# Tying the modulation row sums to the five-tap convolution that precedes them

## Chip, core and metric

The kernel runs on one core of a Trainium2 chip. The metric is the device time of one launch in microseconds (us), the median of three runs. The engines are TensorE (PE, matrix products; PEld is its weight load), VectorE (DVE), ScalarE (ACT), GpSimd (POOL) and SyncE (SP, which here issues most DMA transfers).

## The reference

One layer of a diffusion backbone over 512 latent tokens of width 1024 and 256 context tokens. Cut to its shape:

```
mod = silu(c) @ w_ada + b_ada        # 6 chunks of 1024: shift, scale, gate, shift, scale, gate
h   = modulate(rms_norm(x), shift1, scale1)
z, xbc, dt, conv_in, pool_in, gates = split(h @ w_in)
y_ssd  = bidirectional_ssd(silu(depthwise_conv5(xbc)), softplus(dt + bias)) * silu(z)
y_conv = silu(layer_norm(depthwise_conv31(glu(conv_in))))
y_pool = multi_scale_pool(pool_in)
x = x + gate1 * (merge(y_ssd, y_conv, y_pool, sigmoid(gates)) @ w_out)
x = x + gate2 * swiglu(modulate(rms_norm(x), shift2, scale2))
out = rms_norm(x)
```

The change touches the part of `mod` that isn't needed for `h`: chunks 2, 4 and 3 (gate1, scale2, shift2), 24 row blocks of 128 outputs. Each is a sum over 1024 inputs, `sum(w_ada_row * silu(c)) + b_ada`, worked out on DVE.

## The kernel before

Weights are stored as 128 x 1024 blocks. `load_unit` (L116) brings one in on SP's queue (`wr`, three buffers, L113), ACT casts it to `whi` (L121), DVE takes the rest as `wlo` (L123), and PE multiplies it with the activations in three matmuls per 128 rows (L135 to L137, `mm3`), 24 matmuls of 128x512 for a unit of 512 tokens.

The stages follow one another on PE as: the convolution branch's inputs (`glu_pair`), the pooling branch, the dt block (`dt_all`, L594 on), twelve units of xbc with the five-tap convolution (`conv5`, L673; DVE taps at L677), then the units of z and of the branch gates (`spill_tile`, `gate_tiles`), in which the SSD chunks (`ssd_gen`, L780) are mixed, then the projections `wcv`, `wso`, `wout` and the feed-forward part.

The dt block: DVE makes dt by a chain on tiles of 128x192 (L621 to L624), then dta (L628) and its logs (L631); PE takes dta at L638 to L641 and L655. An SSD chunk: PE makes C.B (L819), ACT copies it (`cbs`, L821), PE applies the states (L832, L836), DVE scales and adds (L833, L837 to L839), masks and multiplies the decays (L854, L857), PE transposes and adds into one bank (`y`, L846 and L859), DVE multiplies with the gate (L866), ACT squares (L868), DVE adds (L869, L870), PE averages (L872).

The 31-tap convolution of the second branch, `conv31` (L391), is 180 steps on DVE (L403) on three pairs of tiles, A_456, A_457 and A_458. `conv_steps` issues so many of them at a place. `cv_norm` (L424) sums the six tiles (`sum`, L427 and L429) and gives the sum to PE (mean matmul L430), which needs one bank for that.

The order is not that of the text. A scheduler takes, on each engine, what its estimate says is ready, by priority; a block under `later(n)` has a lower one. `tc.issue_after(ins)` gives the instructions under it an edge in issue order alone: they come behind `ins` on their engine, and do not wait for its end elsewhere. `mark` is a list that starts with a small copy and to which every five-tap step is appended (L677 to L680); `conv_steps(n, mark[-1])` already uses it for the 31-tap steps.

The 24 row sums are made by `ada`: it first reduces what has been loaded (`ada_rest`, L733, the reduction at L736 with a read of the accumulator), then takes the next row block and loads its 512 KB (`ar`, two buffers, L747, on SP's queue). It is called once in each xbc unit from the fourth on, after `conv_steps`, then once for every second unit in `gate_tiles` and in the `wcv` loop, and in the `wso` loop (there for chunk 5, in `wr` buffers).

Of the kernel before, what the change touches and what calls it, by code (L numbers as in the profile page):

```python
# [11 lines left out]
ALU = mybir.AluOpType  # L12
# [40 lines left out]
def hybrid_block(ctx, tc, x, cx, cck, cc, wad, wada, vec, prm, cst, inv, win, wdt, wcv, wpl, wso, wout, wgu, wdn, out):  # L53
# [10 lines left out]
    V, S, PE = (Ordered(e) for e in (nc.vector, nc.scalar, nc.tensor))  # L64
# [25 lines left out]
    def vc(field, i, n=1):  # L90
        o = VEC_OFF[field] + i
        return vec_t[:, o : o + n]
# [10 lines left out]
    mod_l = per.tile([P, 48], F32, tag="modl", name="mod_l")  # L103
# [235 lines left out]
    V, S, PE = nc.vector, nc.scalar, nc.tensor  # L339
# [216 lines left out]
    silb = [None]  # L556
# [114 lines left out]
    mark = [V.tensor_copy(junk, eps_t)]  # L671
# [61 lines left out]
    def ada_rest():  # L733
        while loaded:
            i, raw = loaded.pop()
            V.tensor_tensor_reduce(raw, raw, silb[0], 1.0, vc("b_ada", i), ALU.mult, ALU.add, mod_l[:, i : i + 1])  # L736

    def ada(n=1):
        for _ in range(n):
            ada_rest()  # L740
            if adas:
                chunk, t = adas.popleft()
                if chunk == 5:
                    raw = load_raw(wada[(chunk - 2) * 8 + t], 1024)
                else:
                    raw = pt(f1, [P, 1024], "ar", 2)
                    nc.sync.dma_start(raw, wada[(chunk - 2) * 8 + t])  # L747
                loaded.append((chunk * 8 + t, raw))
# [189 lines left out]
    for m in range(8):  # L938
        w = load_unit(wso[m])
        o = mmp()  # L940
        for k in range(KT):
            mm3(o, w, k * P, y_hl[k], k == 0, k == KT - 1)
        ga, mo = slot_a(), slot_c().rearrange("p (a b) -> p a b", b=T)
        nc.gpsimd.dma_start(ga, gat[:, m])
        nc.gpsimd.dma_start(mo, mrg[:, m])
        S.activation(ga, ga, AF.Sigmoid)
        V.tensor_tensor(mo[:, 1, :], mo[:, 1, :], ga[:, 1, :], ALU.mult)
        V.tensor_tensor(mo[:, 0, :], mo[:, 0, :], mo[:, 1, :], ALU.add)
        V.tensor_tensor(ga[:, 0, :], o, ga[:, 0, :], ALU.mult)
        V.tensor_tensor(mo[:, 0, :], mo[:, 0, :], ga[:, 0, :], ALU.add)  # L950
        mr = mo[:, 0, :]
        split(mg[m][0], mg[m][1], mr)
        ada(m < 7)
        if m == 7:
            ada_rest()
# [391 lines left out]
```

## Time and profile before

| | us |
|---|---|
| median of three runs | 980.04 (980.01 to 980.17) |
| the profiled execution | 978.48 |
| its span | 976.7 |
| PE busy | 950.0 |
| DVE busy | 764.3 |
| ACT busy | 496.7 |

The span runs from the first to the last instruction; the profiled execution's own time is 1.8 us above it. The rows further down come from this one execution. In the timelines each row is a start, a duration, the engine, the line, the operation and its operands; a bracket gives the idle time of the engine before it and what ended it. Matmuls overlap: the starts tell their pace, not the durations. The granted clock (PEclk) is the share of TensorE's full speed, 1.00 for 2.4 GHz and 0.50 for 1.2 GHz.

### The profile page before, as it was taken

Reading aid. Unit: us, or ns where it says so; the run is one execution under the profiler, and the core shown is the slowest. Engines: PE = TensorE matmul, PEld = TensorE weight load, DVE = VectorE, ACT = ScalarE, POOL = GpSimd, SP = SyncE. Lnnn points to the kernel's source line nnn. Section 1 sums busy time; section 2 is a strip of 40 time slices with the busy share of each in tenths; the row PEclk is TensorE's granted clock in tenths of the full one; section 3 lists DMA queues with packets and bytes.
Section 4 is the critical chain, followed back from the end, with each engine's and each line's share of the span. In section 5 each row is a group of like instructions: output and inputs, shape, how many; then the busy total and the mean of one; then the engine's idle time right before and its main releaser. Section 6 shows DMA issues by size and latency. Waiting matters only on the chain.

```text
span 976.7 us, 14064 instructions
## 1 busy us (share of the span) xinstructions
PE 950.0 (97%) x5340; PEld 802.9 (82%) x5340; DVE 764.3 (78%) x1175; ACT 496.7 (51%) x818; POOL 25.2 (3%) x74
## 2 busy tenths in 40 slices
PE   6999899999999999999999999999999999999996
PEld 4678688887888777667888889989999999888885
DVE  5589899999999999888664764999888888743333
ACT  4684388525444255564844444646555556432331
POOL 0000000000000000000001100000000000000000
PEclk9999899999999999999999999999999999999998
DMA  9777876331112245654557762323232323443422
GB/s 358 307 239 253 272 266 201 129 120 65 66 44 87 98 162 194 187 180 135 188 192 281 238 221 81 104 91 130 89 126 90 109 108 118 150 142 107 137 60 87
DMA packets 55492, 151.67 MB, mean 155 GB/s; under 512 B 5760, under 2 KB 16512, under 8 KB 54272
## 3 DMA queue, kind: packets, MB, share of 16 engines
q1 hardware_dynamic: 53120, 142.38, 42.5%
q0 software_dynamic: 2304, 8.39, 2.5%
q8 instruction: 42, 0.69, 0.3%
q14 instruction: 26, 0.21, 0.1%
HBM read 134.43 MB, written 16.32 MB: 154 GB/s over the span
## 4 chain that ended last, share of the span: by engine, by line
PE 88%; DVE 7%; DMA 2%; issue 1%; ACT 1%; SPq 0%; DVEq 0%; ACTq 0%
PE mm L135 18%; PE mm L137 18%; PE mm L136 18%; PE mm L1134 10%; PE ps L1134 8%; DVE A L403 2%; PE mm L764 2%; PE mm L62 1%; PE ps L1051 1%; PE ps L797 1%; PE ps L62 1%; DVE wlo L123 1%; DVE C L677 1%; DMA E<-cumd 1%; PE mm L765 1%
## 5 line engine op out<-in xcount | busy, mean ns | idle before, releaser
L135 PE MATMUL mm<-hh,whi 128*128 128x512 f32 (+1 forms) x612 | 241.9, 395 | 0.0
L137 PE MATMUL mm<-hh,wlo 128*128 128x512 f32 (+1 forms) x612 | 241.2, 394 | 0.0
L136 PE MATMUL mm<-hl,whi 128*128 128x512 f32 x576 | 229.7, 399 | 0.0
L121 ACT CAST whi<-wr 128x1024 fp32r<-128x1024 f32 (+1 forms) x115 | 116.8, 1019 | 196.9 <-PE mm L136 153.1
L123 DVE TENSOR_TENSOR wlo<-wr,whi 128x1024 fp32r<-128x1024 f32 (+1 forms) x112 | 132.0, 1181 | 62.8 <-ACT whi L121 62.2
L137 PEld LDWEIGHTS mm<-hh,wlo 128*128 128x128 f32 x612 | 115.0, 188 | 28.1 <-issue 3.8
L135 PEld LDWEIGHTS mm<-hh,whi 128*128 128x128 f32 x612 | 115.0, 188 | 27.5 <-issue 2.9
L136 PEld LDWEIGHTS mm<-hl,whi 128*128 128x128 f32 x576 | 108.3, 188 | 24.8 <-issue 3.0
L403 DVE SCALAR_TENSOR_TENSOR A<-U,vec_t,A 128x480 f32<-128x480 f32 (+14 forms) x180 | 116.0, 683 | 2.2 <-ACT A L397 2.2
L1134 PE MATMUL mm<-T,shi 128*128 128x256 f32 x288 | 53.5, 283 | 0.0
L129 ACT CAST shi<-S 128x1024 fp32r<-128x1024 f32 x36 | 37.9, 1052 | 29.1 <-DVE S L1122 23.2
L130 DVE TENSOR_TENSOR slo<-S,shi 128x1024 fp32r<-128x1024 f32 x36 | 44.1, 1224 | 6.2 <-ACT shi L129 6.2
L677 DVE SCALAR_TENSOR_TENSOR C<-C,vec_t,C 128x772 f32<-128x772 f32 (+1 forms) x48 | 46.2, 968 | 0.0
L1134 PEld LDWEIGHTS mm<-T,shi 128*128 128x128 f32 x288 | 44.8, 191 | 0.0
L129 ACT CAST whi<-wr 128x1024 fp32r<-128x1024 f32 (+1 forms) x36 | 30.0, 834 | 27.9 <-PE ps L1134 23.3
L852 ACT ACTIVATE E<-E,sbias 128x128 f32<-128x128 f32 x128 | 40.3, 393 | 6.7 <-DMA E<-cumd 6.7
L130 DVE TENSOR_TENSOR wlo<-wr,whi 128x1024 fp32r<-128x1024 f32 (+1 forms) x36 | 34.5, 957 | 8.8 <-ACT whi L129 7.0
L1134 PE MATMUL mm<-T,slo 128*128 128x256 f32 x144 | 40.9, 284 | 0.0
L736 DVE CUSTOM_DVE_ANT_0 ar<-ar,sil,vec_t 128x1024 f32<-128x1024 f32 x24 | 30.6, 1280 | 8.3 <-DMA ar<-in_wada_dram 8.1
L764 PE MATMUL mm<-H,whi 128*128 128x512 f32 x80 | 28.6, 397 | 0.0
L1134 PE MATMUL ps<-T,shi 128*128 128x256 f32 x144 | 27.6, 289 | 0.6 <-DMA wr<-in_wgu_dram 0.6
L1134 PEld LDWEIGHTS mm<-T,slo 128*128 128x128 f32 x144 | 27.6, 192 | 0.0
(391 smaller groups left out, 2058.0 us busy)
## 6 DMA issues: line engine op xcount, KB each, us to landing
wr<-in_win_dram SPq DMA_DIRECT2D x62, 512.0 KB, 3.8
wr<-in_wgu_dram SPq DMA_DIRECT2D x44, 512.0 KB, 3.4
ar<-in_wada_dram SPq DMA_DIRECT2D x24, 512.0 KB, 4.6
E<-cumd SPq DMA_DIRECT2D x16, 512.0 KB, 5.1
wr<-in_wdn_dram SPq DMA_DIRECT2D x16, 512.0 KB, 3.9
X<-in_wad_dram SPq DMA_DIRECT2D x4, 1024.0 KB, 10.4
H<-in_wad_dram SPq DMA_DIRECT2D x4, 1024.0 KB, 11.0
mrg<-tmp SPq DMA_DIRECT2D x16, 256.0 KB, 3.4
```

What stands on the lines that cost most here:

```text
L121: S.copy(hi[:, :n], raw[:, :n])
L123: V.tensor_tensor(lo[:, :n], raw[:, :n], hi[:, :n], ALU.subtract)
L129: S.copy(dst_hi, src)
L130: V.tensor_tensor(dst_lo, src, dst_hi, ALU.subtract)
L135: PE.matmul(o, hi[:, col : col + P], rh, start=first, stop=False)
L136: PE.matmul(o, hi[:, col : col + P], rl, start=False, stop=False)
L137: PE.matmul(o, lo[:, col : col + P], rh, start=False, stop=last)
L403: V.scalar_tensor_tensor(accs[e][:, :, o], ins[e][:, :, q], vc("dw_w", (2 * j + e) * 31 + 15 + d), accs[e][:, :, o], ALU.mult, ALU.add)
L677: tap = V.scalar_tensor_tensor(a[:, 0:n], pad[:, k : n + k], vc("conv_w", i * 5 + k), a[:, 0:n], ALU.mult, ALU.add)
L764: PE.matmul(oc, w[0][:, ks], hc[k][1], start=k == 0, stop=False, skip_group_check=True)
L852: S.activation(dec[d][:, j, :], dec[d][:, j, :], AF.Identity, bias=sbias[:, z, c : c + 1])
L1134: PE.matmul(o[:, left], x[:, cs], rhs[k][y], start=first and k + n == 0, stop=k == 3 and n == 2, skip_group_check=True,)
```

## The change

The reduction of `ada_rest` is put under `tc.issue_after(mark[-1].ins)`, `mark[-1]` being the last five-tap step recorded when `ada_rest` is called.

```
     def ada_rest():
         while loaded:
             i, raw = loaded.pop()
-            V.tensor_tensor_reduce(raw, raw, silb[0], 1.0, vc("b_ada", i), ALU.mult, ALU.add, mod_l[:, i : i + 1])
+            with tc.issue_after(mark[-1].ins):
+                V.tensor_tensor_reduce(raw, raw, silb[0], 1.0, vc("b_ada", i), ALU.mult, ALU.add, mod_l[:, i : i + 1])
```

The same instructions are issued; their order differs. On DVE, around the end of the dt chain, before (`ar` is a loaded row block, W_861 the polynomial's tile, `dts` is dt, W_841 takes dta, `wlo` is a weight's rest):

```order
L123 TENSOR_TENSOR wlo_1135<-wr_1132,whi_1134 128x1024
L621 SCALAR_TENSOR_TENSOR W_861<-W_861,W_865 128x192
L736 ISA ar_3725,mod_l<-ar_3725,sil_460,vec_t 128x1024
L736 ISA mod_l 128x1
L622 SCALAR_TENSOR_TENSOR W_861<-W_861,W_857 128x192
L736 ISA ar_3784,mod_l<-ar_3784,sil_460,vec_t 128x1024
L736 ISA mod_l 128x1
L624 SCALAR_TENSOR_TENSOR dts<-W_861,W_855 128x192
L994 SCALAR_TENSOR_TENSOR m_l<-mod_l,vec_t 128x8
L403 SCALAR_TENSOR_TENSOR A_456<-U_505,vec_t,A_456 128x8x62
L628 SCALAR_TENSOR_TENSOR W_841<-dts,W_841 128x96
```

And the same end of the chain in the changed kernel:

```order
L123 TENSOR_TENSOR wlo_1090<-wr_1087,whi_1089 128x1024
L621 SCALAR_TENSOR_TENSOR W_861<-W_861,W_865 128x192
L403 SCALAR_TENSOR_TENSOR A_456<-U_505,vec_t,A_456 128x8x58
L622 SCALAR_TENSOR_TENSOR W_861<-W_861,W_857 128x192
L403 SCALAR_TENSOR_TENSOR A_456<-U_502,vec_t,A_456 128x8x57
L624 SCALAR_TENSOR_TENSOR dts<-W_861,W_855 128x192
L403 SCALAR_TENSOR_TENSOR A_456<-U_505,vec_t,A_456 128x8x57
L628 SCALAR_TENSOR_TENSOR W_841<-dts,W_841 128x96
```

The reductions have left the chain, 31-tap steps stand in their places, and the chain ends behind an earlier split (wlo_1090 in place of wlo_1135).

On PE, the dt block's first matmuls (ps_884) before, within the unit mm_1093:

```order
L135 MATMUL mm_1093<-hh_83,whi_1089 128x512
L136 MATMUL mm_1093<-hl_84,whi_1089 128x512
L638 MATMUL ps_884<-W_841,W_839 128x4x16
L639 MATMUL ps_884<-W_841,W_839 128x6x16
L640 MATMUL ps_884<-W_841 128x16
```

And in the changed kernel:

```order
L136 MATMUL mm_1017<-hl_96,whi_1013 128x512
L137 MATMUL mm_1017<-hh_95,wlo_1014 128x512
L638 MATMUL ps_884<-W_841,W_839 128x4x16
L639 MATMUL ps_884<-W_841,W_839 128x6x16
L640 MATMUL ps_884<-W_841 128x16
```

The block stands at the end of mm_1017 now; the whole unit mm_1050 and five matmuls of mm_1093 come behind it.

On PE, around the mean matmul of the convolution branch (mm_3326) before; `ps_4346` to `ps_4371` belong to one SSD chunk, `mm_3210` and `mm_3244` are units of the gates:

```order
L137 MATMUL mm_3210<-hh_95,wlo_3207 128x512
L135 MATMUL mm_3244<-hh_81,whi_3240 128x512
L430 MATMUL mm_3326<-sum_3327,mean 128x512
L872 MATMUL ps_4346<-W_4342,mean 128x128
L819 MATMUL ps_4356<-ct,bt 128x128
L832 MATMUL ps_4367<-H_2635,ct 128x512
L836 MATMUL ps_4371<-pinit,ct 128x512
L136 MATMUL mm_3244<-hl_82,whi_3240 128x512
```

And in the changed kernel (`ps_4279` to `y_4309` are of the chunk before that one):

```order
L137 MATMUL mm_3244<-hh_95,wlo_3241 128x512
L873 MATMUL ps_4279<-W_4275,mean 128x128
L820 MATMUL ps_4289<-ct,bt 128x128
L833 MATMUL ps_4300<-H_2616,ct 128x512
L837 MATMUL ps_4304<-pinit,ct 128x512
L847 MATMUL y_4309<-ident,W_4299 128x128 x4
L860 MATMUL y_4309<-E_4285,X_1680 64x128 x8
L430 MATMUL mm_3326<-sum_3327,mean 128x512
L873 MATMUL ps_4346<-W_4342,mean 128x128
L820 MATMUL ps_4356<-ct,bt 128x128
L833 MATMUL ps_4367<-H_2635,ct 128x512
L837 MATMUL ps_4371<-pinit,ct 128x512
```

Both chunks' pieces stand behind the last matmul of mm_3244, one after the other; before, those of the first chunk stood within mm_3173 and mm_3210.

On DVE at the same place in the changed kernel (W_4299 is the operand of y_4309, A_458 the last pair of 31-tap tiles):

```order
L839 TENSOR_TENSOR W_4299<-W_4299,W_4297 128x512
L403 SCALAR_TENSOR_TENSOR A_458<-U_2474,vec_t,A_458 128x8x50
L840 TENSOR_TENSOR W_4299<-W_4299,W_4303 128x512
L403 SCALAR_TENSOR_TENSOR A_458<-U_2477,vec_t,A_458 128x8x50
...
L403 SCALAR_TENSOR_TENSOR A_458<-U_2474,vec_t,A_458 128x8x49
L867 TENSOR_TENSOR W_4283<-y_4309,W_4283 128x512
L429 TENSOR_TENSOR sum_3327<-sum_3327,A_458 128x512
L403 SCALAR_TENSOR_TENSOR A_458<-U_2477,vec_t,A_458 128x8x49
L870 TENSOR_TENSOR W_4342<-W_4342 128x256
L429 TENSOR_TENSOR sum_3327<-sum_3327,A_458 128x512
```

Between L840 and L867 stand six 31-tap steps, and the sum's last add comes behind the chunk's L867 and behind the split wlo_3443; before, it stood between the splits wlo_3207 and wlo_3241.

## Rows read from the trace of the kernel before

**Rows 1.** Page, part 1: busy time, share of the span and instructions of each engine.
```profile
PE 950.0 (97%) x5340; PEld 802.9 (82%) x5340; DVE 764.3 (78%) x1175; ACT 496.7 (51%) x818; POOL 25.2 (3%) x74
```

**Rows 2.** Waits of PE: line waited, for what: us in total, times, longest.
```profile
PE ps L638 <- issue: 3.9, 1, 3.9
PE ps L797 <- DVE W L795: 1.3, 2, 1.0
...
PE ps L695 <- ACT bt L690: 1.0, 1, 1.0
```

**Rows 3.** Page, part 5: the reductions' group (busy, mean ns; idle before, releaser).
```profile
L736 DVE CUSTOM_DVE_ANT_0 ar<-ar,sil,vec_t 128x1024 f32<-128x1024 f32 x24 | 30.6, 1280 | 8.3 <-DMA ar<-in_wada_dram 8.1
```

**Rows 4.** Timeline of DVE at the end of the dt chain.
```profile
112.95 1.28 DVE L736 CUSTOM_DVE_ANT_0 ar<-ar,sil,vec_t 128x1024 f32<-128x1024 f32 x1 [1.31 <-DMA ar<-in_wada_dram]
...
114.17 0.35 DVE L624 SCALAR_TENSOR_TENSOR dts<-W,W 128x192 f32<-128x192 f32 x1
...
114.51 0.73 DVE L403 SCALAR_TENSOR_TENSOR A<-U,vec_t,A 128x496 f32<-128x496 f32 x1
115.16 0.25 DVE L628 SCALAR_TENSOR_TENSOR W<-dts,W 128x96 f32<-128x96 f32 x1
```

**Rows 5.** Timeline of PE around the dt block.
```profile
111.03 0.39 PE L135 MATMUL mm<-hh,whi 128*128 128x512 f32 x1
111.26 0.40 PE L136 MATMUL mm<-hl,whi 128*128 128x512 f32 x1
115.51 0.66 PE L638 MATMUL ps<-W,W 128*128 128x64 f32 x2 [3.86 <-issue]
...
122.05 0.51 PE L137 MATMUL mm<-hh,wlo 128*128 128x512 f32 x1
```

**Rows 6.** Windows there: length, busy time by engine, PEclk, DMA share, GB/s.
```profile
111.50:115.50 4.00, 0.15 (x1) 0.02 (x1) 2.69 (x9) 2.12 (x3) 0.00 (x0) 0.93 0.88 331
115.50:121.50 6.00, 5.99 (x27) 4.97 (x28) 4.01 (x11) 2.60 (x4) 0.00 (x0) 0.50 0.72 242
...
122.00:125.00 3.00, 3.00 (x15) 2.44 (x14) 3.00 (x6) 2.24 (x4) 0.31 (x1) 1.00 0.29 89
```

**Rows 7.** Windows: PE, PEld, DVE, ACT and POOL busy ahead of the sum.
```profile
303.00:427.00 124.00, 122.07 (x586) 91.73 (x586) 120.59 (x191) 62.93 (x129) 7.67 (x5) 1.00 0.48 155
```

**Rows 8.** Timeline of PE, one SSD chunk and the mean matmul, projection matmuls left out.
```profile
438.01 0.39 PE L819 MATMUL ps<-ct,bt 128*128 128x128 f32 x2
...
444.20 0.63 PE L846 MATMUL y<-ident,W 128*128 128x128 f32 x4
444.75 1.09 PE L859 MATMUL y<-E,X 128*64 128x128 f32 x16
...
447.96 1.02 PE L430 MATMUL mm<-sum,mean 128*128 128x512 f32 x2
448.82 0.38 PE L872 MATMUL ps<-W,mean 128*128 128x128 f32 x2
```

**Rows 9.** Timeline of DVE around the sum's last add.
```profile
422.31 1.15 DVE L403 SCALAR_TENSOR_TENSOR A<-U,vec_t,A 128x392 f32<-128x392 f32 x2
...
426.31 0.69 DVE L429 TENSOR_TENSOR sum<-sum,A 128x512 f32<-128x512 f32 x1
...
427.52 1.22 DVE L857 TENSOR_TENSOR E<-E,cbs 128x1024 f32<-128x1024 f32 x1
...
428.80 0.68 DVE L833 TENSOR_TENSOR W<-ps,dte 128x512 f32<-128x512 f32 x1
429.40 0.68 DVE L837 TENSOR_TENSOR W<-ps,dte 128x512 f32<-128x512 f32 x1
```

**Rows 10.** Windows around two short waits of PE in the feed-forward stage.
```profile
650.00:654.00 4.00, 2.23 (x17) 1.85 (x16) 4.00 (x6) 2.62 (x4) 0.00 (x0) 1.00 0.42 150
654.00:658.00 4.00, 4.00 (x23) 4.00 (x23) 2.98 (x4) 0.16 (x1) 0.00 (x0) 0.57 0.30 115
```

**Rows 11.** Page, part 6: the row blocks' loads, KB each, us to landing.
```profile
ar<-in_wada_dram SPq DMA_DIRECT2D x24, 512.0 KB, 4.6
```

## Prediction

> **What bounds the kernel now.** I read the shares of the engines first, then what TensorE (PE) waits for, then the stretches around those waits, and last VectorE (DVE). Lines are those of the kernel before; in the changed file lines behind L735 stand one lower. PE is busy 950.0 of 976.7 us [rows 1], so the time is PE's work plus what opens between two of its matmuls. One of its few waits bears on this change at once: 3.9 us at L638, the first matmul of the dt block [rows 2]. The view names "issue" as releaser; the timelines show the real one: L638 starts at 115.51, right behind the L628 at 115.16 that makes its operand [rows 4, 5]. Ahead of that, DVE runs reductions (L736), one of which waited 1.31 us for its load while L624, which needs no load, stood behind it [rows 4]. The 24 reductions take 1280 ns each, and DVE is idle 8.1 us in all for their loads [rows 3].
>
> That wait costs more than itself. PE issues its last matmul before it at 111.26 and the next large one at 122.05 [rows 5], where the cadence of such matmuls is 0.23 us. The granted clock is 0.50 from 115.5 to 121.5 and 1.00 from 122 [rows 6]: the lower level, 1.2 GHz, for some 6 us. The dt block, 115.51 to 122.05, takes 6.54 us there and would take 3.27 at 2.4 GHz. So the place costs 122.05 - 111.49 - 3.27 = 7.3 us: 4.0 of waiting and 3.3 of clock.
>
> The second place has no wait yet. Around 438 to 449 PE runs ends of SSD chunks (L819, L832, L836, then L846 and L859, then L872) and the mean matmul of the convolution branch, L430, at 447.96 [rows 8]. From L819 to L846 lie 6.2 us in which DVE and ScalarE (ACT) make L846's operand; PE fills them with projection matmuls that stand in between. L430 needs the last add (L429) of the channel sum, which starts at 426.31 [rows 9]: 21 us of slack. DVE has next to none: 120.59 of 124 us busy from 303 to 427 [rows 7].
>
> **The change part by part.** Two DVE instructions in a row overlap by some 0.08 us [rows 4, 9], so each counts its duration less that.
>
> *The early stretch loses its reductions.* Both kernels issue the same instructions. In front of the split wlo_1090 no reduction stands now, where 12 stood, and 16 more conv steps (L403) and 3 more L621 do: 12 x 1.28 = 15.4 us less against 16 x 0.65 + 3 x 0.27 = 11.2 more, and no wait for a load. PE's dt block moves too, from behind the fifth matmul of mm_1093 to the end of mm_1017, 29 matmuls or 6.6 us earlier: PE comes to it at 111.49 - 6.6 = 104.9. Is its operand there? wlo_1090 waits for its cast on ACT, which PE paces and which stays where it was, at 99.4 to 100.4. From there DVE runs wlo_1090 (1.14), L621, L622 and L624 (0.27 each), three L403 (0.65 each) and L628 (0.17): 4.1 us, 104.5. So L638 waits 0 to 0.5 us and nothing is there to drop the clock. Gain 6.8 to 7.3; I take -7.1. The 1.0 us at L695 [rows 2], where ACT stands behind five-tap work of DVE, goes too, with 7 to 9 us less DVE work ahead of it: -1.0 (0 to -1.0).
>
> *Where they go.* 18 of the 24 now stand behind wlo_2657, the rest between the five-tap units. In front of that split DVE has 18 x 1.28 = 23 us less and 7 L403, 4.2 us, more. It can't use these 19 us to run ahead, as each split waits for a cast that PE paces. Behind it the work comes back: in front of the last L429 stand, against before, 4 more splits (4 x 1.13 = 4.5), two more chunk ends (L833, L837, L838, L839, L866 at 0.6 each, L857 1.14, L869 0.35: 9.0), and one L854, L795, L799 with small ones (3.5): 17 us more. So from wlo_2657 to the sum DVE has 36 us more to do, where it was 97% busy. By DVE's work alone, the sum of 427.0 comes at 427.0 + 36 - 8 (PE arrives that much earlier) = 455.
>
> *What PE does there.* In the changed PE order L872, L819, L832, L836, L846, L859, L430 and the next chunk's L872 to L836 stand back to back behind the last matmul of mm_3244, with no projection matmul among them. PE meets DVE's chain bare. First wait, for L846: from L819's start ACT's copy (0.78), then on DVE L824 (0.22), L857 (1.14), L825 (0.14), L833, L837, L838 (0.6 each), L839 (0.68) and two L403 (0.56 each): 5.9, less PE's own 1.95 for L819 to L836: 4.0; with the 6.2 of [rows 8] 4.2; up to 5.1 where DVE comes late to L824. I take 4.4. Second wait, for L430: behind L839 stand six L403 (6 x 0.57 = 3.4), L866 (0.6), L429 (0.6), L403 (0.56), L869 (0.35) and L429 (0.68): 6.2, less 1.6 for L846 and L859 on PE: 4.6; at least 3.0, what lies between the end of L859 at 445.8 and the L872 that hangs on it [rows 8]. Ahead of both, L872 waits 0 to 0.9; I take 0.4. Together 9.4 us (7.0 to 10.9). None of it is hidden: the ready projection matmuls are queued on PE behind the waiting ones. In the new place and with nothing waiting, L430 would run 23 matmuls later than before, at 447.96 + 23 x 0.229 = 453.2; less 8.1 plus 9.4 is 454.5, and DVE's own 455 agrees. So the cluster gives back all that was won, and 1.3 us more.
>
> *The clock there.* Two places price a wait: 3.9 us idle was followed by 6.5 us at the lower level, a loss of 3.3 [rows 5, 6]; 1.8 us idle within four by four at 0.57, a loss of 4 x 0.43 = 1.7 [rows 10]. The two new waits are nearest the first. If the first of them drops the clock, it is L846 and L859 that slow, from 1.6 to 3.2 us, beside six L403 of 3.4, which costs nothing; the stretch behind the second wait is then paid once: +3.2 (0 to 6.6).
>
> *The loads.* 22 of the 24 go on SP's queue from among the first weights to between the weights of the five-tap stage and behind them: 11.5 MB out of a stretch with a DMA share of 0.72 to 0.88 [rows 6]. With two ar buffers a load starts when the reduction two before is done, and weight loads stand behind it on SP. It lands after 4.6 us at the median [rows 11], and reductions stand 4 us or more apart. Where DVE waits for one, all behind it waits too: +0, at most +4.
>
> Sum: -7.1 - 1.0 + 9.4 + 3.2 + 0 = +4.5. The profiled execution, 978.48, becomes 983.0; it lies 1.56 under the median of the runs, 980.04, to which the same step gives **984.5**.
>
> **Rivals.** A measurement of this kernel tells 0.2%, 2 us, from no change.
> 1. *Faster, 977.* DVE passes the split wlo_3443 well before PE ends mm_3244. Then L872 doesn't wait, the two waits are at their lower ends (4.0 and 3.0) and the clock holds; the 1.3 us at L797 [rows 2], a wait for the same kind of DVE work, goes as well: -8.1 - 1.3 + 7.0 = -2.4, or 977.6, and 976 if a part of the six L403 runs ahead too. It decides at DVE's time at that split: before some 439 (453.2 - 8.1 less 3.9 for the pieces between, and 2 us) it holds. For it: by work alone DVE is there at 455 - 13 = 442, with 3 us of doubt. Against it: the row that shows it 97% busy.
> 2. *No change, 981.3.* The clock holds at both waits: +1.3. For it: the view of L695's 1.0 us names no loss behind it. Against it: rows 6 and 10.
> 3. *Clock paid twice, 988.* If the clock doesn't come back between the two waits, the low stretch is as long as two: 2 x 3.3 = 6.6, 987.9. The Trainium skill, "TensorE: Matmul & The Clock Gate", section "HAM oscillation — how this bites in real kernels", describes a loop whose waits drop the clock in every pass, so that every pass pays anew; by that rule this rival holds. The traces here show single waits, after each of which the price was paid once.
> 4. *Gain not had, 992.* The dt chain is still late, so 7.1 stays lost; PE comes later to the cluster, but its waits are the chain's own: -1.0 + 9.4 + 3.2 = 11.6, 991.6. Against it: the 4.1 us of the chain hold no load.
> That the reductions stay where they were is excluded by the changed order.
>
> **How the numbers follow.** Forecast 0.43 (982 to 987), rival 1 0.20, rival 2 0.15, rival 3 or late loads 0.15, rival 4 0.07. Faster by over 0.2% is rival 1: 0.20; within it are rival 2 and the lower edge of the forecast: 0.18; slower 0.62. The range takes in rival 1 and rival 3 with a part of the late loads: 976 to 990; the forecast's own is 982 to 987.
>
> **What would show it.** Right: no wait at L638 and a clock of 1.00 from 100 to 125; reductions from some 125 to 370 us; two PE waits of 4 to 5 us, at L846 and L430, near 445 to 455, and a clock of 0.5 behind them. Wrong: a wait at L638 above 1 us; L430's wait under 2 us; no fall of the clock near 455; or DVE idle for ar loads by more than 3 us between 125 and 370.

## Result and profile after

The changed kernel takes 986.89 us (median of four runs, 985.63 to 987.51), the kernel before, run beside it, 980.02. The ratio is 1.0089, with a 95% interval of 1.0067 to 1.0111: slower by about 0.9%, where 984.5 was forecast, in a range of 976 to 990. The profiled execution of the changed kernel took 987.3 us, 8.8 more than that of before; this gap is what the traces can explain. Lines of the changed file behind L735 are one higher than those of before.

The page's first part, the answer to [rows 1]: PE and DVE have the same work as before, in a longer span of 985.5 us.

```profile
PE 951.9 (97%) x5340; PEld 804.0 (82%) x5340; DVE 766.2 (78%) x1175; ACT 493.8 (50%) x816; POOL 29.0 (3%) x74
```

What PE waits for (line waited, for what: us in total, times, longest), the answer to [rows 2]:

```profile
PE ps L62 <- DMA X<-in_wad_dram: 8.3, 2, 7.2
PE ps L798 <- DVE W L796: 5.2, 4, 2.8
PE y L847 <- DVE W L840: 4.7, 1, 4.7
PE mm L430 <- DVE sum L429: 2.9, 1, 2.9
```

The first wait is the start's, as before. L638 and L695 have left the list; L847 and L430 have come, and L798 (L797 before, 1.3 us) has grown to 5.2.

The dt block, timeline of PE and the window around it, the answers to [rows 5] and [rows 6]:

```profile
103.99 0.33 PE L638 MATMUL ps<-W,W 128*128 128x64 f32 x2
...
105.64 1.92 PE L655 MATMUL ps<-W,W 128*16 128x128 f32 x16
```

```profile
100.00:125.00 25.00, 25.00 (x125) 20.63 (x124) 23.48 (x42) 17.65 (x38) 0.62 (x2) 1.00 0.56 202
```

No bracket stands at L638, PE is busy for all 25 us, and the granted clock (last column but two) is 1.00. The reductions moved as the order said, only later than I had put them, from 231 us on and not from 125: duration (min, median, max), first and last start, and DVE's idle time for their loads, which was 8.1 us [rows 3]. Fourteen of the 24 start between 331 and 381 us.

```profile
L737 DVE CUSTOM_DVE_ANT_0 ar<-ar,sil,vec_t x24: 1267/1278/1464, 230.9 to 381.2; 128x1024 f32<-128x1024 f32 x24
...
DMA ar<-in_wada_dram: 2.1, 4
```

The pieces of the two SSD chunks, timeline of PE, the answer to [rows 8]:

```profile
447.48 1.02 PE L837 MATMUL ps<-pinit,ct 128*128 128x512 f32 x2
453.19 1.08 PE L847 MATMUL y<-ident,W 128*128 128x128 f32 x4 [4.70 <-DVE W L840]
454.21 1.98 PE L860 MATMUL y<-E,X 128*64 128x128 f32 x16
459.05 2.07 PE L430 MATMUL mm<-sum,mean 128*128 128x512 f32 x2 [2.87 <-DVE sum L429]
...
464.40 0.96 PE L135 MATMUL mm<-hh,whi 128*128 128x512 f32 x1
```

The same place in windows (length, busy time of PE, PEld, DVE, ACT, POOL, PEclk, DMA share, GB/s):

```profile
445.80:448.50 2.70, 2.56 (x9) 1.12 (x8) 2.37 (x6) 1.82 (x4) 0.00 (x0) 1.00 0.48 146
448.50:451.50 3.00, 0.00 (x0) 0.00 (x0) 3.00 (x6) 0.00 (x0) 1.31 (x1) 0.93 0.64 216
451.50:459.00 7.50, 2.99 (x20) 2.29 (x20) 7.50 (x15) 0.63 (x1) 0.00 (x0) 0.50 0.14 38
459.00:465.30 6.30, 6.25 (x12) 3.31 (x13) 4.31 (x10) 1.58 (x4) 1.21 (x1) 0.54 0.14 38
465.30:470.00 4.70, 4.70 (x23) 3.82 (x22) 4.16 (x7) 1.71 (x3) 0.14 (x1) 1.00 0.00 0
```

PE does nothing for 3 us while DVE is busy throughout, the clock falls to 0.50 (1.2 GHz of 2.4), is back at 1.00 only after 465, and DVE is full in the window between: the two waits are DVE's chain, met bare.

A third place is new. From 340 to 400 us, first before, then after:

```profile
340.00:400.00 60.00, 59.18 (x285) 44.58 (x284) 58.82 (x95) 30.79 (x62) 4.09 (x2) 1.00 0.53 173
```

```profile
340.00:400.00 60.00, 55.05 (x261) 41.54 (x260) 53.99 (x86) 29.68 (x60) 3.97 (x2) 0.97 0.76 250
```

PE loses 4.1 us of busy time there, and DVE loses 4.8 too: it isn't fuller but emptier, while the DMA share rises from 0.53 to 0.76. This is the stretch of three of the four waits at L798, 5.0 of the 5.2 us. DVE's and ACT's waits there in the changed kernel, then ACT's wait for E before:

```profile
DVE cbj L825 <- ACT cbs L822: 3.0, 2, 2.1
DVE ar L737 <- DMA ar<-in_wada_dram: 1.8, 3, 0.8
ACT E L853 <- DMA E<-cumd: 9.1, 4, 3.6
```

```profile
ACT E L852 <- DMA E<-cumd: 1.0, 1, 1.0
```

The loads reach PE on two ways. ACT stands at a load of E (from which a chunk's decays are made), and the copy `cbs` behind it comes late to DVE; and DVE itself stands at row blocks. The longest wait at L798, 2.8 us, ends at 375.6 with the product of an L796 that DVE runs at 374.9; in the 21 us ahead of it DVE stood 0.9 us for `cbs` and 1.8 us for row blocks.

To see where time goes and comes from, the n-th matmul of hh or hl into an mm bank is looked up in two timelines; the difference of the starts is what was lost up to there. Read from the traces, in us (before, after, and of four experiments the difference to before):

```
   n   before    after  diff | e3_noload e7_small e11_bytes e12_mix
   0    24.02    23.16  -0.9 |   -0.9      -0.4     +0.6     -0.6
 336   126.53   118.60  -7.9 |   -7.9      -7.5     -6.5     -7.7
 768   250.46   241.41  -9.1 |   -9.1      -8.7     -7.6     -8.0
1104   369.51   361.62  -7.9 |   -8.2      -5.6     -6.2     -7.7
1152   383.67   379.73  -3.9 |   -7.5      -4.1     -5.8     -7.2
1296   440.42   429.24 -11.2 |  -13.6      -6.2     -8.1     -8.8
1440   481.03   489.73  +8.7 |   +5.1      -2.2     -5.7     -6.4
2300   933.55   942.30  +8.8 |   +5.2      -2.7     -5.7     -6.3
```

Between 1152 and 1440 the SSD pieces stand at other matmuls in each kernel, so single rows there mislead; at 1440 they are all behind. The dt block gives 7.1 us (from -0.9 to -7.9), the first xbc units 1.1 more, and everything is lost from 350 to 480.

### The profile page after: what moved, and what is told of

It is laid out like the page before. It is cut to its first block, busy times and chain, and to the rows that moved or that the text cites. A ratio compares the mean times of both kernels' runs of the same rounds, so it can differ in the third digit from the quotient of the medians.

```text
span 985.5 us, 14060 instructions
## 1 busy us (share of the span) xinstructions
PE 951.9 (97%) x5340; PEld 804.0 (82%) x5340; DVE 766.2 (78%) x1175; ACT 493.8 (50%) x816; POOL 29.0 (3%) x74
## 4 chain that ended last, share of the span: by engine, by line
PE 86%; DVE 7%; DMA 4%; issue 1%; ACT 1%; SPq 0%; DVEq 0%
PE mm L135 18%; PE mm L137 18%; PE mm L136 18%; PE mm L1135 10%; PE ps L1135 8%; DMA ar<-in_wada_dram 2%; PE mm L765 2%; PE mm L62 1%; PE ps L1052 1%; PE ps L798 1%; PE mm L766 1%; PE ps L62 1%; PE ps L723 1%; DVE wlo L123 1%; DVE A L403 1%
## 5 line engine op out<-in xcount | busy, mean ns | idle before, releaser
L136 PE MATMUL mm<-hl,whi 128*128 128x512 f32 x576 | 229.1, 398 | 0.0
L136 PEld LDWEIGHTS mm<-hl,whi 128*128 128x128 f32 x576 | 108.3, 188 | 25.3 <-issue 3.3
L403 DVE SCALAR_TENSOR_TENSOR A<-U,vec_t,A 128x504 f32<-128x504 f32 (+14 forms) x180 | 115.4, 677 | 4.6 <-ACT A L397 4.6
```

The source lines that it names most:

```text
L136: PE.matmul(o, hi[:, col : col + P], rl, start=False, stop=False)
L403: V.scalar_tensor_tensor(accs[e][:, :, o], ins[e][:, :, q], vc("dw_w", (2 * j + e) * 31 + 15 + d), accs[e][:, :, o], ALU.mult, ALU.add)
```

## Experiments

The kernel before ran beside each group of experiments again, with medians of 978.0 to 978.6 us, against 980.0 at first; so ratios are compared, and a time is read against the kernel before that ran beside it. The changed kernel itself was repeated once:

> The changed kernel once more, on the chip of the other runs of this call, as the reference for them: 986 to 987.5, ratio 1.007 to 1.011 to the kernel before.

986.05 us, ratio 1.009 (1.0069 to 1.011): the same result. Its trace has the same waits, 5.0 us at L798, 4.7 at L847 and 3.3 at L430.

**Where the gain comes from: e1_dt.** The reductions tied to the end of the dt chain.

```
-            V.tensor_scalar(lnd[:, d], d4[:, d, 0:4], 1e-37, None, ALU.max)
+            dt_end.append(V.tensor_scalar(lnd[:, d], d4[:, d, 0:4], 1e-37, None, ALU.max))
...
-            with tc.issue_after(mark[-1].ins):
+            with tc.issue_after(dt_end[-1].ins):
```

> The changed kernel, but the 24 reductions are tied to the last step of the dt chain (the L631 of the second direction) in place of the last five-tap step; so they start near 105 us, behind the chain, and on DVE the last add of the channel sum stands again between the splits wlo_3207 and wlo_3241; on PE the SSD pieces have projection matmuls between them. Theory A (the gain is the dt chain without reductions, the loss is the late work on DVE): the wait at L638 is gone (7.1) and nothing is lost later: 980.0 - 7.1 = 973, with L695 and L797 up to 2 less: 971 to 974. Rival B (the reductions cost their time wherever DVE is busy, and early work only moves the wait on): PE waits for DVE between 105 and 300 instead, 978 to 981.

974.59 us, ratio 0.9964 (0.9947 to 0.9981), which on the 980.0 of the first runs is 976.5, between the two forecasts. The gain at L638 is there in full, 7.1 us in the trace, so it hangs on the reductions' leaving the dt chain and not on where they go. Rival B is right in part: DVE is short of time behind the chain as well, and PE's waits from 100 to 300 us show it.

```profile
PE ps L697 <- ACT bt L692: 2.7, 2, 1.5
PE ps L136 <- DVE C L130: 1.6, 1, 1.6
```

The operand of L136 comes at 181.4, behind a reduction and a split that DVE began at 179.1; the wait at L697 was not followed further. Some 3.8 us of the gain are given back before 250 us.

**The bare pieces: e2_g6.** One gate pair more ahead of the convolution branch's norm, so that projection matmuls stand between the pieces again.

```
-GATES_BEFORE_LN = 5
+GATES_BEFORE_LN = 6
```

> The changed kernel with one gate pair more in front of the convolution branch's norm (GATES_BEFORE_LN 6 in place of 5). Reductions, loads and their DVE order up to 400 us stay; on PE the SSD chunks' ends get projection matmuls between them again, and L430 comes one unit later. Theory A (12 us of the loss are the two bare waits and the clock behind them, 5 us are earlier): 986.9 - 12 = 975, no clock below 0.9 near 450, the waits at L798 near 345 to 395 stay at 5 us. Rival C (DVE's work is the bound, and the place on PE matters little): PE waits as long for the sum one unit later, 984 to 987.

976.62 us, ratio 0.9983 (0.9971 to 0.9995), 10.4 us below the changed kernel's 1.0089 (1.06% of 978.4). L847 and L430 have left the list of waits, and the clock is whole:

```profile
440.00:480.00 40.00, 39.38 (x202) 29.30 (x201) 36.52 (x64) 15.96 (x27) 2.35 (x2) 1.00 0.51 159
```

Rival C falls: with 20 projection matmuls between the pieces, DVE's same work costs next to nothing. The kernel before was not run with this gate pair; it had nothing to gain there, as its PE is busy for all of the 40 us from 440 to 480. The waits at L798 stay, as expected:

```profile
PE ps L798 <- DVE W L796: 6.0, 3, 2.3
```

**The clock: e4_fill.** The first wait filled with matmuls that nobody reads.

```
+            if (g, z) == FILL:
+                with tc.issue_after(last.ins):
+                    for _ in range(NFILL):
+                        PE.matmul(y.rearrange("p a b -> p (a b)"), ident, xtok[:, z, gs], start=True, stop=True)
```

> The changed kernel with five matmuls of 128x512 (two passes, 0.86 us each at the full clock) that nobody reads, in front of L847 of the one chunk where PE waits 5.06 us; they write into the bank that L847 overwrites, so the wait is filled and nothing else is added. Behind it on PE the next chunk's L873 to L837 stand ahead of L430 now. Theory F (the idle time drops the clock, and the clock is 3 to 4 us of the loss): the clock stays at 1.00 through L847 and L860; if the next wait, 3 to 5 us at L873 or L430, then drops it by itself, the stretch at 0.5 begins there and is about 7 us long in place of 13.5, and the time is 985 to 987; if it does not, 982.5 to 984. Rival G (the clock falls whatever PE does there): 13 us at 0.5 and 987 to 988.

987.16 us, ratio 1.0094 (1.0075 to 1.0114). Windows behind the fill:

```profile
454.00:456.00 2.00, 1.68 (x5) 0.40 (x3) 2.00 (x5) 0.00 (x0) 0.00 (x0) 1.00 0.00 0
456.00:458.00 2.00, 1.66 (x20) 1.25 (x20) 2.00 (x4) 0.00 (x0) 0.00 (x0) 1.00 0.00 0
458.00:460.00 2.00, 0.00 (x0) 0.00 (x0) 2.00 (x5) 0.63 (x1) 0.00 (x0) 1.00 0.18 55
460.00:462.00 2.00, 0.94 (x5) 0.97 (x6) 1.97 (x5) 0.27 (x1) 0.00 (x0) 0.84 0.78 205
462.00:464.00 2.00, 2.00 (x3) 0.77 (x3) 1.83 (x6) 0.27 (x1) 0.00 (x0) 0.50 0.01 2
464.00:466.00 2.00, 2.00 (x5) 0.87 (x4) 1.38 (x3) 0.00 (x0) 1.04 (x1) 0.80 0.00 0
```

With PE fed, the clock stays at 1.00 through the y block (L847 and L860); rival G falls. Then a wait of 3.4 us for the sum of L871 (L877 in that file) lowers it by itself, for some 4 us in place of 13.5, as theory F had it in its first case (there with about 7).

```profile
PE ps L879 <- DVE W L877: 3.4, 1, 3.4
```

The time hardly moves. The trace's loss over the pieces is 18.5 us in place of 19.9 (from n = 1296 to behind them), and the waits at L798 were 7.1 in that run in place of 5.2. So the low clock between the two waits was nearly free here: DVE's steps cover it, and the price is paid behind the last wait. This is one run, and the order of the pieces behind the fill is not that of the changed kernel.

**The third place: loads or DVE's work?** First, without 22 of the loads.

```
+                    if len(kept) < 2:
+                        kept.append(pt(f1, [P, 1024], "ar", 2))
+                        nc.sync.dma_start(kept[-1], wada[(chunk - 2) * 8 + t])
+                    raw = kept[t % 2]
```

> The changed kernel, but only the first two of the 24 row blocks are loaded; the other reductions run on those two tiles again, so 11.5 MB of loads are left out (part of the computation is left out) and DVE's work stays. It tells what holds DVE and PE from 345 to 395 us, where PE waits 5.2 us at L798. Theory D (the loads: each of the last reductions waits for its own, and other transfers on SP wait behind them): PE's waits at L798 fall to 1 to 2 us and the time to 982 to 983. Rival E (the reductions' own 1.28 us each on a full DVE): the waits stay at 4 to 5 us and the time at 986 to 987.

985.08 us, ratio 1.0072 (1.0055 to 1.009). In the median that is 1.7 us less than the changed kernel, in the traces 3.6 (table above, +5.1 against +8.7). From 340 to 400 us:

```profile
340.00:400.00 60.00, 58.77 (x277) 42.98 (x276) 58.21 (x94) 32.71 (x70) 5.28 (x3) 1.00 0.53 175
```

DVE's work is all there, PE has all but 0.4 us of its busy time again, and L798's waits (L801 in that file) are down to 0.2 us. So by the waits theory D holds and E falls: at this place it is the loads. By the time it isn't shown: 1.0072 lies within the interval of the changed kernel's 1.0089, and the 3.6 us are those of one pair of executions, the slowest but one of the changed kernel's four and the fastest of this one's. The bare pieces remain, with waits of 3.3, 2.6 and 2.1 us.

Next, the reductions cut to a sixteenth and the loads kept.

```
-                V.tensor_tensor_reduce(raw, raw, silb[0], 1.0, ...
+                V.tensor_tensor_reduce(raw[:, 0:64], raw[:, 0:64], silb[0][:, 0:64], 1.0, ...
```

> The changed kernel, each of the 24 reductions made over the first 64 of its 1024 columns (part of the computation is left out); all loads stay, in the same places among SP's other transfers. It takes 24 x 1.2 = 28 us off DVE and nothing off DMA. Theory A (DVE's work is the root; the loads cost only because a full DVE waits behind them): PE's waits at L798 fall under 2 us, the SSD pieces have matmuls between them, the early gain of 8 us stays: 971 to 974. Rival D (the loads alone make the 5 us from 345 to 395, through the transfers that wait behind them): L798 still waits 3 to 5 us, 975 to 978.

976.82 us, ratio 0.9989 (0.9978 to 1.0). I had expected theory A; rival D came true:

```profile
PE ps L798 <- DVE W L796: 4.9, 3, 2.1
```

With 28 us less on DVE the scheduler put 16 and 19 projection matmuls between the pieces, and they no longer stand bare; this is worth 10 us by ratios, as in e2_g6. But the waits at L798 are as long as with the whole reductions.

Both single steps together, one gate pair more and no loads:

> Both single steps at once: one gate pair more in front of the norm, and only two of the 24 row blocks loaded (the other reductions run on those two again; part of the computation is left out). Theory (the two losses are of separate origin and add): the first took 10 us off the changed kernel, the second 3.6, together 13 to 14: 987 - 13.5 = 973.5, 5 to 7 us under the kernel before. If they are one loss seen twice: 976 to 978, no better than the first alone.

974.66 us, ratio 0.9957 (0.9944 to 0.997), its profiled execution 971.63. By ratios the two steps took 1.06% and 0.17% singly and 1.32% together: two losses that add, within the width of the intervals. With the gate pair the loads cost 0.26%, 2.5 us, and the two intervals (0.9971 to 0.9995 and 0.9944 to 0.997) no longer meet.

What is it about the loads? They wait on SP for a reduction, with E's loads for ACT behind them, and they are 11.5 MB. Two runs put one or the other on GpSimd's queue (both with the gate pair of e2_g6):

```
-                nc.sync.dma_start(
+                nc.gpsimd.dma_start(
                     dec[d].rearrange("p h l -> p (h l)"),
```

> The changed kernel with one gate pair more in front of the norm (as in e2_g6) and the 16 E loads (cumd, 512 KB each) issued on GpSimd's queue in place of SP's; the 24 row blocks stay on SP. It tells how the loads hold PE from 345 to 395 us. Theory J (order on SP's queue: a row block's load waits there for a reduction, and the E load behind it comes late to ACT): ACT's waits for E fall from 18 to under 8 us, PE's waits at L798 from 6.0 to 2, and the time to 972 to 974, as without the loads. Rival K (the bytes: 11.5 MB more in a stretch with a DMA share of 0.75 make every transfer there late): ACT still waits 12 us or more for E, L798 4 us or more, 976 to 978.

```
-                    nc.sync.dma_start(raw, wada[(chunk - 2) * 8 + t])
+                    nc.gpsimd.dma_start(raw, wada[(chunk - 2) * 8 + t])
```

> The changed kernel with one gate pair more in front of the norm, and the 24 row blocks loaded on GpSimd's queue in place of SP's; the E loads stay on SP. Theory J (order on SP's queue): the same gain as in e9_Epool_g6, 972 to 974, unless GpSimd's own products (L829) come late behind a waiting load, which DVE's L839 would show. Rival K (the bytes): 976 to 978.

986.88 us (ratio 1.0083) and 985.05 (1.0071): both some 9 to 10 us worse than e2_g6, which neither theory had. GpSimd's queue has waits of its own, and they hold the loads behind them. In e9 ACT waits 31.2 us for E in place of 18.4, and PE 12.1 at L798 in place of 6.0; in e10 ACT waits 9.7, but GpSimd stands 135.9 us at the row blocks' loads, waiting for reductions, and PE at L798 8.1. So these two don't part order from bytes. That E came late isn't the whole cause, since in e10 it came early and the waits grew.

The run that parts them keeps every load in its place on SP and makes it small, beside the small reductions of e7:

```
-                    nc.sync.dma_start(raw, wada[(chunk - 2) * 8 + t])
+                    nc.sync.dma_start(raw[:, 0:64], wada[(chunk - 2) * 8 + t][:, 0:64])
```

> As e7_small (each reduction over the first 64 of 1024 columns), and each row block's load brings those 64 columns alone: 32 KB in place of 512 (part of the computation is left out). The loads stay where they are on SP, and each still waits there for the reduction two before it; 11.8 MB are gone. It parts the order on SP from the bytes, which the two runs on GpSimd's queue did not. Theory K (the bytes: every transfer from 345 to 395 us comes late): ACT's waits for E fall from 14.9 to 8 us or less, PE's waits at L798 from 4.9 to 2 or less, time 972 to 974. Theory J (the order on SP): both stay, 976 to 978.

972.24 us, ratio 0.9942 (0.9918 to 0.9966). PE's waits there, in e11 alone:

```profile
PE ps L798 <- DVE W L796: 1.0, 2, 0.7
PE ps L798 <- ACT whi L121: 0.9, 1, 0.9
```

SP still stands long before these loads, 54.8 us against 58.1 in e7_small:

```profile
SPq L748 <- DVE mod_l L737: 54.8, 11, 6.6
```

Of the 4.9 us, 1.9 are left; the order on SP stayed and the bytes went. So it is the bytes, theory K, and by ratio they cost 0.47%, 4.6 us, from e7_small to this run, with intervals that don't meet. The landing times show how. Loads of weights and of E from 340 to 400 us (count, KB each, median us to landing), weights before and in the changed kernel:

```profile
wr<-in_win_dram SPq DMA_DIRECT2D x8, 512.0 KB, 3.5
```

```profile
wr<-in_win_dram SPq DMA_DIRECT2D x8, 512.0 KB, 5.6
```

And both in e7_small, then in e11:

```profile
wr<-in_win_dram SPq DMA_DIRECT2D x8, 512.0 KB, 4.4
E<-cumd SPq DMA_DIRECT2D x5, 512.0 KB, 5.7
```

```profile
wr<-in_win_dram SPq DMA_DIRECT2D x8, 512.0 KB, 3.7
E<-cumd SPq DMA_DIRECT2D x6, 512.0 KB, 3.8
```

One expectation of K was missed: ACT's wait for E fell from 14.9 to 11.2 us only, not to 8. What part of the remaining E waits is order was not tried further. The PE order of e11 also differs from that of e7 in where some chunk pieces stand, which I can't hold fixed; the waits at L798 fall on the same steps.

**Is there a better place? e5_late.** All 24 behind the branch's norm.

```
-        ada(q > 2)
...
-            ada(m % 2)
+            ada(2 + (m == 0))
```

> The changed kernel with the reductions moved on: no row block is asked for in the xbc and gate units, two in each wcv unit (three in the first) and one in each of seven wso units, and the reductions are tied to the last step of the convolution branch's norm (L439) in place of the last five-tap step. So all 24 run behind some 470 us, where DVE was busy 9 to 20 of 25 us; gate1 is needed near 580. Between 105 and 470 DVE has 30 us less to do than in either kernel. Theory A (the early gain is the chain without reductions, the loss is late work on a full DVE): the gain of 7 to 8 us stays, no wait above 1 us follows: 971 to 973. Rival H (DVE or DMA work in the projections binds there: wso and wout wait for gates or for weights behind the loads on SP): waits of PE at L135 to L137 or L972 between 500 and 600, 975 to 980.

982.68 us, ratio 1.0054 (1.0036 to 1.0072): rival H, and above its range. The early gain is there (-7.5 at n = 336), some 2.7 us go from 280 to 480, which was not followed further, and the rest, 7.8 us, is lost in the projections. PE's waits from 500 to 600 us, what DVE waits for there, and the window from 525 to 550 in this run, then in the kernel before:

```profile
PE mm L137 <- DVE wlo L123: 4.0, 4, 1.4
PE mm L135 <- ACT W L129: 1.6, 1, 1.6
DVE ar L737 <- DMA ar<-in_wada_dram: 11.4, 6, 5.8
```

```profile
525.00:550.00 25.00, 23.66 (x101) 18.46 (x100) 16.60 (x24) 11.07 (x13) 3.30 (x7) 1.00 0.91 337
```

```profile
525.00:550.00 25.00, 25.00 (x111) 20.51 (x110) 17.29 (x25) 13.20 (x15) 4.75 (x9) 1.00 0.91 327
```

Idle time of DVE was not the same as room: before, DVE is free for 7.7 of these 25 us, but the other transfers alone bring the DMA share to 0.91. With the row blocks among them DVE stands 11.4 us at reductions whose block has not landed, and the splits wait behind them.

**e12_mix.** Eight behind the dt chain, eight in the xbc units, eight behind the norm.

```
+            with tc.issue_after((mark if early_done else dt_end)[-1].ins):
...
+    ada(8)
+    ada_rest()
+    early_done.append(1)
```

> The reductions in three groups of eight: the first tied to the end of the dt chain (105 to 150 us), the second one to an xbc unit and tied to its last five-tap step, the third in the wso units, tied to the last step of the branch's norm. Theory: the changed kernel lost nothing up to 300 us with one reduction to a unit (8 us ahead of the kernel before, there); with all 24 behind the dt chain 4 us were lost at the first xbc units, with all 24 behind the norm 5 us from 300 on and 8 in the projections. In groups of eight each place has room: 971 to 974, 5 to 8 us under the kernel before. Rival: eight are too many in the first place or the last: 975 to 978.

972.54 us, ratio 0.994 (0.9917 to 0.9963): 0.6% faster than the kernel before, and faster than the changed one. It isn't shown to be faster than e1_dt (0.9964), whose interval meets this one. No wait of PE between 100 and 600 us is longer than 1.5 us, and PE is busy for 98 of the 100 us from 300 to 400:

```profile
300.00:400.00 100.00, 98.22 (x459) 74.09 (x458) 97.58 (x156) 45.29 (x89) 5.26 (x4) 1.00 0.46 146
```

## Why the prediction was right, and which term was mis-sized

The direction and the two mechanisms were right; the sum of +4.5 stands against +6.9 in the medians and +8.8 in the profiled executions, and 986.9 lies just inside the forecast's own 982 to 987. By its own steps:

- *Dt block, -7.1.* Measured -7.1 (from -0.9 at the start to -7.9 at n = 336). L638 doesn't wait, the clock is 1.00. e1_dt and e12_mix keep this gain with other ties.
- *L695, -1.0.* Measured -1.1 (-7.9 to -9.1 at n = 768).
- *The bare pieces, 9.4.* The waits are 0.3 ahead of L873, 4.7 and 2.9: 7.9. The second is shorter than my 4.6 because L847 and L860 took 3.0 us at half clock, in place of 1.6: wait and work together are 5.9, where I had 6.2. What I took to stand in one term went into the slowed work, as the prediction said it would. (The upper end of the sum's range for this term, 10.9, is a slip: 5.1, 4.6 and 0.9 make 10.6.)
- *The clock, 3.2.* Behind the second wait 6.3 us ran at 0.54, a loss of 2.9. With 1.4 for the slowed y block, pieces and clock make 12.2, against 12.6 in the sum. e2_g6, which takes both away, is 10.4 us faster by ratios.
- *The loads, 0 with an upper end of 4.* This is the term that was mis-sized. I took the reductions to stand 4 us or more apart, so that a load had time to land; fourteen of them stand within 50 us, some pairs 1.6 to 2.1 us apart. I asked whether DVE would wait for the row blocks; it did so for 2.1 us. I did not ask what nine of them, 4.6 MB, would do to the other transfers from 340 to 400 us, where the share already was 0.53. These landed later, weights after 5.6 us in place of 3.5, ACT waited 9.1 us for E in place of 1.0, and PE paid at L798: 5.2 us of waits (1.3 before), and a granted clock of 0.50 from 376 to 378. The clock is not part of it each time: in e6_after the same wait is 1.5 us long and the stretch has 1.00. The rest of the sum puts the term at 5: -7.1 - 1.1 + 12.2 + 0.8 (small drift from n = 768 to 864) leaves 4.8 of a total of 9.6 from the start's -0.9. That is this one execution; the repeat loses 7.9 from its start's value on, in place of 9.6. Without the loads 3.6 us go in the trace of e3_noload, 1.7 in its median (not clear of noise) and 2.5 from e2_g6 to e8_g6noload; e11_bytes shows that it is the bytes. So the term is 2 to 5 us, not 0, and its upper end of 4 was about right.
- *DVE's time for the sum, 455.* It was ready at 459.0 (L429 at 458.31, 0.68 long), four late. That the loads' delay was handed on here is not shown: in e3_noload, without the loads and with another order of the pieces, the sum is ready no earlier, at 460.0.

Of the rivals, 1, 2 and 4 are excluded: the split wlo_3443 ran at 446.84, not before 439; the clock fell; the dt gain was had. Rival 3, the clock paid twice, named nearly the time (988), and its condition was met: the clock didn't come back between the two waits. But it was not paid twice, since the work between the waits was covered by DVE's steps. By the rule of the Trainium skill ("TensorE: Matmul & The Clock Gate", "HAM oscillation — how this bites in real kernels"), that each wait throws the clock back for the next pass, the trace of e4_fill agrees: there the second wait, 3.4 us, lowered it alone. A slow stretch cost here only where nothing else covered it: of 13.5 us at half clock some 6 lay behind the last wait and cost about 3, and shortening the stretch to 4 gained no more than 1.4.

For the loads, the Trainium skill, "DMA: Bandwidth & Descriptors", section "Issuing engines are not separate DMA queues", states that transfers of all issuing engines end up on the same 16 DMA engines, so that another issuer saves only the time it takes to start them. The runs e9 and e10, in which another issuer helped nothing (1.0083 and 1.0071), agree with it, though their loss has a cause of its own, the waits on GpSimd's queue. Had I weighed the bytes against [rows 7], where the share is 0.48 without the row blocks, they would have been a term.

## What to carry to other kernels

A wait taken out of an early chain is a gain one can price from the timeline; but the work that made it must run somewhere, and each new place has to be asked two things apart: is there time on the engine, and is there room for its loads among the transfers that others wait for. Before trusting slack on the engine order, look for places where small dependent pieces stand back to back on PE without large matmuls among them: there the whole chain of the other engine is exposed, however early it is elsewhere. And moved work can be split: three groups of eight gave 0.994, where 24 in one place gave 0.9964 behind the dt chain, 1.0054 behind the norm and 1.0089 in the changed kernel. Against the last two the split is clearly better, against the first it isn't shown.

## What was not expected of the hardware

The granted clock, once lowered at 451, stayed at 0.50 through some 3 us of matmuls between two waits and rose only at 465; with the first wait filled by matmuls that nobody reads it stayed at 1.00 until the second. A DMA share of 0.76, far from 1, was enough to raise the landing time of a 512 KB load of weights from 3.5 to 5.6 us (5.2 in the repeat, 4.4 in e7_small at 0.75) and to reach PE through two other engines. And GpSimd's queue, though GpSimd is busy for 4% of the span in e10, was a worse place for the row blocks than SP's full one: it stood 135.9 us at waits of these loads, and DVE's waits for them grew from 2.5 us in e2_g6 to 8.8.
